# First weight pieces of the second pair issued on ScalarE's queue, layer 1's parameters loaded on the sync queue behind the lead

## The chip, the cores and the metric

The kernel runs on one core of one Trainium2 chip. The metric is the device time of one execution in microseconds (us). Before the change it was measured three times: 1794.83 us in the median, 1794.76 to 1796.19 us from end to end.

## What is computed

A trunk of two layers over 512 tokens of width 1024, all in float32. Each layer adds half of a SwiGLU feed-forward block, then a mixer (a convolution group beside differential attention, with one input and one output projection), then half of a second SwiGLU block:

```python
def rms_norm(x, g):
    xf = x.astype(jnp.float32)
    y = xf * lax.rsqrt(jnp.mean(xf * xf, axis=-1, keepdims=True) + EPS)
    return (y * g.astype(jnp.float32)).astype(x.dtype)

def swiglu(h, w_gate, w_up, w_down):
    return (jax.nn.silu(h @ w_gate) * (h @ w_up)) @ w_down

for l in range(DEPTH):
    x = x + 0.5 * swiglu(rms_norm(x, ffn1_norm[l]), ffn1_w_gate[l], ffn1_w_up[l], ffn1_w_down[l])
    h = rms_norm(x, mix_norm[l])
    ...
    x = x + jnp.concatenate([conv_out, diff_out], axis=-1) @ w_out[l]
    x = x + 0.5 * swiglu(rms_norm(x, ffn2_norm[l]), ffn2_w_gate[l], ffn2_w_up[l], ffn2_w_down[l])
```

D_FF is 2816, DEPTH is 2. The change lies in the first microseconds of layer 0's first `swiglu`.

## The kernel before

`x` is held transposed, as eight tiles of 128 features by 512 tokens (`x[:, k, :]`, k from 0 to 7). A product in float32 precision is made from three matmuls in the fp32r type: each operand is split into a high part and a rest, and `mm3` (L169 to L176) adds high by high (L172), rest of the activations by high weights (L175) and high activations by rest of the weights (L176). Weights come as raw float32 tiles `wraw`; `parts_of` (L96 to L101) makes their high part `whi` on ScalarE (L100; for the very first piece on VectorE, L98) and their rest `wlo` on VectorE (L101). `Prep.tile` (L258) does the same for the activations with the gain from the parameters: `acth` on ScalarE (L260), `actl` on VectorE (L261). The normalising factor is applied to the products afterwards, so the matmuls can start before it is known.

The first two of the 22 feed-forward blocks of 128 features are the lead. Each has a gate and an up weight tile, so there are four tiles of 128 by 1024 (512 KB), numbered n = 0 to 3 in the loop of L203; n = 0 and 1 are the first pair, n = 2 and 3 the second. The load loop of L200 brings them in three cuts: columns of k = 0 alone (64 KB for each tile), k = 1 to 3 (192 KB each), k = 4 to 7 (256 KB each), with the tiles of `x` between them. `lead_products` (L292) runs over k and, in each k, over the four tiles with three matmuls each: 12 matmuls for a k, 96 for the lead. Nine matmuls on ones (`ps_idle`, L196) run ahead of them, while the first data is on its way.

Plain loads are issued by SyncE (`nc.sync`) in program order, except the two parameter tables (`pars`, one for each layer, 128 by 159), which ScalarE issues first of all (L188). After them ScalarE loads its function table and runs one tiny activation on ones (L193). GpSimd issues the small loads of `make_scalars` and `make_bias` (L511, L491), which prepare scalars of both layers: they read `pars[0]` and `pars[1]` (L531, L535, L539, L542) and the table `lamv` (L517, multiplied on L519, reduced on VectorE, L521).

A scheduler places the instructions of each engine in an order that it computes from a model of their durations, so moving a load can reorder the instructions that use it. Each engine then works in its order, and an instruction that waits holds all behind it. Loads issued by SyncE and ScalarE share eight semaphores in turn, so a load's issue waits until the eighth load before it has landed.

Of the kernel before, what the change touches and what calls it, by code (L numbers as in the profile page):

```python
# [19 lines left out]
DEPTH = 2  # L20
# [47 lines left out]
def trunk(ctx: ExitStack, tc: tile.TileContext, xt, par, lamv, relb, onehot,  # L68
          gu1, dn1, wag, wqkv, wout, gu2, dn2, out):
    nc = tc.nc  # L70
# [25 lines left out]
    def parts_of(raw, hi, lo, eng=None, first=False):  # L96
        if first:
            V.tensor_scalar(hi, raw, 1.0, None, op0=ALU.mult)  # L98
        else:
            S.activation(hi, raw, AF.Copy)  # L100
        (eng or V).tensor_tensor(out=lo, in0=raw, in1=f32(hi), op=ALU.subtract)  # L101
# [81 lines left out]
    pars = []  # L183
    for l in range(DEPTH):
        pt = const.tile([P, NPAR], F32, tag=f"par{l}", name=f"par{l}")
        pars.append(pt)
    for l in range(DEPTH):
        nc.scalar.dma_start(pars[l], par[l])  # L188

    ones_r = const.tile([P, P + SPACE], F32R, tag="ones_r", name="ones_r")[:, :P]  # L190
    V.memset(f32(ones_r), 1.0)
# [8 lines left out]
    for k0, k1 in ((0, 1), (1, 4), (4, KT)):  # L200
        h = slice(k0 * P, k1 * P)
        nc.sync.dma_start(x[:, k0, :], xt[k0])
        for n, (raw, hi, lo) in enumerate(lead):  # L203
            nc.sync.dma_start(raw[:, h], gu1[0, n // 2, n % 2][:, h])
            parts_of(raw[:, h], hi[:, h], lo[:, h], first=k0 == n == 0)
        for k in range(k0 + 1, k1):
            nc.sync.dma_start(x[:, k, :], xt[k])
    lead = [[tuple(t[1:]) for t in lead[2 * m : 2 * m + 2]] for m in range(2)]
    ident = const.tile([P, P], F32, tag="ident", name="ident")
    make_identity(nc, ident)  # L210
# [725 lines left out]
```

## Time and profile before

| what | us |
|---|---|
| median of 3 runs | 1794.83 |
| lowest, highest | 1794.76, 1796.19 |
| profiled execution, its own time | 1795.22 |
| profiled execution, span from first to last instruction | 1793.4 |
| TensorE busy | 1783.9 |
| VectorE busy | 1199.0 |
| ScalarE busy | 896.4 |
| GpSimd busy | 646.6 |

The profiled execution is one run with the profiler; 1.8 us of its own time lie outside the span of its instructions, and its own time is 0.4 us above the median of the three. The granted TensorE clock was full throughout. In the rows below, PE is TensorE's matmuls, PEld its weight loads, DVE VectorE, ACT ScalarE, POOL GpSimd and SP SyncE; a "q" behind the engine marks what its sequencer issues. Rows of the timeline give the start, the duration from the first to the last of a merged group, the engine, the line, the operation with output and inputs, the count, and in brackets the idle time of the engine ahead of it with what ended it.

### The profile page before, as it was taken

What the parts mean: (1) busy time and instruction counts of PE and PEld (TensorE: products, weight loads), DVE (VectorE), ACT (ScalarE), POOL (GpSimd) and SP (SyncE); (2) the same over time, 40 slices, a digit from 0 to 9 for tenths busy, and PEclk for the clock granted to TensorE, in tenths of its full rate; (3) what the DMA queues carried; (4) which work ended last, traced back from release to release, by engine and by line L of the source; (5) the groups of instructions that cost most, each with busy time, mean ns of one, the idle gap of its engine ahead of it and who ended that gap; (6) DMA issues with size and microseconds to landing.
All of it is one profiled execution on the core that took longest, in us unless ns stands there. A gap on an engine that the chain in (4) does not pass through costs nothing.

```text
span 1793.4 us, 28370 instructions
## 1 busy us (share of the span) xinstructions
PE 1783.9 (99%) x10861; PEld 1590.7 (89%) x10861; DVE 1199.0 (67%) x1849; ACT 896.4 (50%) x1483; POOL 646.6 (36%) x453
## 2 busy tenths in 40 slices
PE   9999999999999999999999999999999999999999
PEld 7899899888788899899888998998887888998997
DVE  6966477568867867467566764765788587674762
ACT  6455265445744456256433543654558354552651
POOL 2243243269843133142102312412798331322420
PEclk9999999999999999999999999999999999999999
DMA  7376466323212366466334654663231133664751
GB/s 246 103 182 180 112 162 191 116 96 94 71 48 83 94 165 189 106 171 190 104 95 98 168 170 120 175 182 117 71 116 50 48 106 92 169 175 108 182 152 59
DMA packets 111721, 231.24 MB, mean 129 GB/s; under 512 B 12151, under 2 KB 33414, under 8 KB 111584
## 3 DMA queue, kind: packets, MB, share of 16 engines
q1 hardware_dynamic: 91488, 191.93, 33.2%
q0 software_dynamic: 19808, 37.33, 12.5%
q8 instruction: 85, 1.39, 0.3%
q14 instruction: 52, 0.43, 0.1%
q10 hardware_dynamic: 288, 0.16, 0.0%
HBM read 227.26 MB, written 3.42 MB: 129 GB/s over the span
## 4 chain that ended last, share of the span: by engine, by line
PE 95%; DVE 3%; issue 1%; DMA 0%; ACT 0%; SPq 0%; ACTq 0%; DVEq 0%
PE ps_pair L384 38%; PE ps_d L172 9%; PE ps_d L175 9%; PE ps_d L176 9%; PE ps_pair L176 5%; PE ps_pair L175 5%; PE ps_pair L172 5%; PE ps_pair L602 2%; PE ps_pair L601 2%; PE ps_pair L600 2%; PE ps_out L175 1%; PE ps_sc L718 1%; PE ps_out L176 1%; PE ps_out L172 1%; DVE actl L261 1%; PE ps_v L632 1%
## 5 line engine op out<-in xcount | busy, mean ns | idle before, releaser
L100 ACT ACTIVATE whi<-wraw 128x512 fp32r<-128x512 f32 (+2 forms) x600 | 466.4, 801 | 610.9 <-PE ps_pair L384 226.7
L101 DVE TENSOR_TENSOR wlo<-wraw,whi 128x512 fp32r<-128x512 f32 (+2 forms) x557 | 516.5, 950 | 225.3 <-ACT whi L100 220.6
L384 PE MATMUL ps_pair<-acth,wlo 128*128 128x256 f32 x1088 | 307.9, 283 | 0.0
L384 PE MATMUL ps_pair<-actl,whi 128*128 128x256 f32 x1088 | 307.9, 283 | 0.0
L384 PE MATMUL ps_pair<-acth,whi 128*128 128x256 f32 x1088 | 307.9, 283 | 0.0
L175 PE MATMUL ps_d<-hl,whi 128*128 128x512 f32 x704 | 274.0, 389 | 0.0
L176 PE MATMUL ps_d<-hh,wlo 128*128 128x512 f32 x704 | 272.9, 389 | 0.0
L172 PE MATMUL ps_d<-hh,whi 128*128 128x512 f32 x704 | 269.1, 389 | 0.0
L384 PE MATMUL ps_pair<-th,wlo 128*128 128x256 f32 x816 | 230.9, 283 | 0.0
L384 PE MATMUL ps_pair<-tl,whi 128*128 128x256 f32 x816 | 230.8, 283 | 0.0
L384 PE MATMUL ps_pair<-th,whi 128*128 128x256 f32 x816 | 230.8, 283 | 0.0
L150 POOL DMA_DIRECT2D wraw<-in_gu x68 | 81.9, 1204 | 408.3 <-DMA wraw<-in_gu 158.2
L155 POOL TENSOR_TENSOR wraw<-wraw 128x512 f32<-128x512 f32 x68 | 108.2, 1591 | 329.6 <-DMA wraw<-in_gu 242.8
L384 PEld LDWEIGHTS ps_pair<-acth,whi 128*128 128x128 f32 x1088 | 208.9, 192 | 0.3
L384 PEld LDWEIGHTS ps_pair<-actl,whi 128*128 128x128 f32 x1088 | 208.9, 192 | 0.3
L384 PEld LDWEIGHTS ps_pair<-acth,wlo 128*128 128x128 f32 x1088 | 208.9, 192 | 0.0
L484 DVE SCALAR_TENSOR_TENSOR x<-ps_d,x 128x512 f32<-128x512 f32 x96 | 64.8, 689 | 180.5 <-PE ps_d L176 180.1
L175 PE MATMUL ps_pair<-actl,whi 128*128 128x512 f32 x448 | 174.8, 391 | 0.3
L172 PE MATMUL ps_pair<-acth,whi 128*128 128x512 f32 x448 | 173.8, 392 | 1.3 <-ACT whi L100 1.3
L176 PE MATMUL ps_pair<-acth,wlo 128*128 128x512 f32 x448 | 174.3, 390 | 0.0
L384 PEld LDWEIGHTS ps_pair<-tl,whi 128*128 128x128 f32 x816 | 156.5, 192 | 0.7
L384 PEld LDWEIGHTS ps_pair<-th,whi 128*128 128x128 f32 x816 | 156.5, 192 | 0.6
(169 smaller groups left out, 3248.7 us busy)
## 6 DMA issues: line engine op xcount, KB each, us to landing
wraw<-in_gu SPq DMA_DIRECT2D x208, 256.0 KB, 4.0
wraw<-in_gu SPq DMA_DIRECT2D x104, 512.0 KB, 3.7
wraw<-in_gu POOLq DMA_DIRECT2D x68, 512.0 KB, 5.7
wraw<-in_wqkv SPq DMA_DIRECT2D x24, 512.0 KB, 3.7
wraw<-in_dn SPq DMA_DIRECT2D x84, 128.0 KB, 3.0
wraw<-in_dn SPq DMA_DIRECT2D x32, 256.0 KB, 3.2
wraw<-in_wag SPq DMA_DIRECT2D x16, 512.0 KB, 3.6
wraw<-in_wout SPq DMA_DIRECT2D x16, 512.0 KB, 3.6
```

The costliest lines, as they stand in the source:

```text
L100: S.activation(hi, raw, AF.Copy)
L101: (eng or V).tensor_tensor(out=lo, in0=raw, in1=f32(hi), op=ALU.subtract)
L150: nc.gpsimd.dma_start(two.rearrange("p (b c) -> p b c", b=2), u[:, h[0]].unsqueeze(1).broadcast_to([P, 2, 512]), accum_op=ALU.add)
L155: G.tensor_tensor(more[:, h[0]], two[:, h[1]], whole[:, h[0]], op=ALU.add)
L172: first = T.matmul(ps, wh, xh, start=start, stop=False)
L175: T.matmul(ps, wh, xl, start=False, stop=False)
L176: T.matmul(ps, wl, xh, start=False, stop=stop)
L384: mm = T.matmul(ps, l, r, start=first and i == j == 0, stop=False, skip_group_check=True)
L484: V.scalar_tensor_tensor(x[:, m, :], ps, 0.5, x[:, m, :], op0=ALU.mult, op1=ALU.add)
L600: T.matmul(ps[n], xh[:, t], wh, start=k == 0, stop=False)
L601: T.matmul(ps[n], xh[:, t], wl, start=False, stop=False)
L602: T.matmul(ps[n], xl[:, t], wh, start=False, stop=k == KT - 1)
```

## The change

Layer 0's parameters stay the first load on ScalarE's queue; layer 1's are issued by SyncE behind the last load of the lead. The first cuts (k = 0) of the two tiles of the second pair (n = 2 and 3) are issued on ScalarE's queue. In the program they come behind ScalarE's table load and its activation on ones.

```diff
-    for l in range(DEPTH):
-        nc.scalar.dma_start(pars[l], par[l])
+    nc.scalar.dma_start(pars[0], par[0])
...
     for k0, k1 in ((0, 1), (1, 4), (4, KT)):
         h = slice(k0 * P, k1 * P)
         nc.sync.dma_start(x[:, k0, :], xt[k0])
         for n, (raw, hi, lo) in enumerate(lead):
-            nc.sync.dma_start(raw[:, h], gu1[0, n // 2, n % 2][:, h])
+            (nc.scalar if k0 == 0 and n > 1 else nc.sync).dma_start(raw[:, h], gu1[0, n // 2, n % 2][:, h])
             parts_of(raw[:, h], hi[:, h], lo[:, h], first=k0 == n == 0)
         for k in range(k0 + 1, k1):
             nc.sync.dma_start(x[:, k, :], xt[k])
+    nc.sync.dma_start(pars[1], par[1])
```

No instruction of an engine is added or taken away; the number and the bytes of the loads stay the same.

## The prediction

> **What bounds the kernel now.** I read the page's first part, then TensorE's waits over the whole run, then the timeline of the first microseconds engine by engine.
>
> ```profile
> PE 1783.9 (99%) x10861; PEld 1590.7 (89%) x10861; DVE 1199.0 (67%) x1849; ACT 896.4 (50%) x1483; POOL 646.6 (36%) x453
> ```
>
> ```profile
> PE ps_at L739 <- ACT at L741: 1.3, 4, 0.4
> PE ps_pair L172 <- ACT whi L100: 1.3, 2, 0.9
> ```
>
> TensorE is busy for 99% of the span, and of its few waits only the second row lies in what the change touches: matmuls of the lead that wait for ScalarE to split a weight piece. TensorE's timeline shows where:
>
> ```profile
> 1.04 4.03 PE L196 MATMUL ps_idle<-ones_r 128*128 128x512 f32 x9 [1.04 <-DVE relb L493]
> 4.92 0.40 PE L172 MATMUL ps_pair<-acth,whi 128*128 128x512 f32 x1
> 5.70 0.50 PE L172 MATMUL ps_pair<-acth,whi 128*128 128x512 f32 x1 [0.38 <-ACT whi L100]
> ...
> 10.14 0.50 PE L172 MATMUL ps_pair<-acth,whi 128*128 128x512 f32 x1 [0.91 <-ACT whi L100]
> 10.48 0.39 PE L175 MATMUL ps_pair<-actl,whi 128*128 128x512 f32 x1
> 10.71 0.40 PE L176 MATMUL ps_pair<-acth,wlo 128*128 128x512 f32 x1
> 11.07 0.50 PE L172 MATMUL ps_pair<-acth,whi 128*128 128x512 f32 x1
> 11.42 0.40 PE L175 MATMUL ps_pair<-actl,whi 128*128 128x512 f32 x1
> ...
> 29.16 0.39 PE L172 MATMUL ps_pair<-acth,whi 128*128 128x512 f32 x1
> ```
>
> The matmul at 29.16 is the first after the lead's 96. Seventeen of the 96 ran before 11.07, so 79 ran from 11.07 on, and from 11.42 to 29.16 there are 78 steps in 17.74 us: 0.2274 us each, with no gap. The one at 11.07 took 0.35 to the next, 0.12 over a step, as does each that comes after a wait. From 4.92 to 29.16 are 24.24 us, and 96 steps are 21.83 us. **2.4 us is therefore all that the lead's waits cost**, 0.13% of the run. Everything behind 29.16 is TensorE's own queue and moves as a block.
>
> Now who is late. ScalarE's timeline:
>
> ```profile
> 0.72 0.89 ACTq L188 DMA_DIRECT2D par<-in_par  x2
> 1.65 1.28 ACT L193 ACT_TABLE_LOAD   x1 [1.65 <-PEq L925]
> 2.94 0.20 ACT L193 ACTIVATE warm<-ones_r 128x1 f32<-128x1 f32 x1
> 3.98 0.72 ACT L260 ACTIVATE acth<-x,par 128x512 fp32r<-128x512 f32 x1 [0.83 <-DMA par<-in_par]
> 5.33 0.88 ACT L100 ACTIVATE whi<-wraw 128x128 fp32r<-128x128 f32 x3 [0.64 <-DMA wraw<-in_gu]
> ...
> 7.79 0.51 ACT L100 ACTIVATE whi<-wraw 128x384 fp32r<-128x384 f32 x1
> 9.56 0.52 ACT L100 ACTIVATE whi<-wraw 128x384 fp32r<-128x384 f32 x1 [1.26 <-DMA wraw<-in_gu]
> 10.50 1.01 ACT L100 ACTIVATE whi<-wraw 128x384 fp32r<-128x384 f32 x2 [0.41 <-DMA wraw<-in_gu]
> ```
>
> Layer 0's parameters end the wait at 3.98; the k = 0 piece of n = 1 lands at 5.3; the 384-column pieces of n = 1 and n = 2 land at 9.55 and 10.5. These last two set the restart at 10.14 and the dense stretch from 11.07. SyncE's issues and the load on the DMA engines:
>
> ```profile
> 0.73 0.39 SPq L202 DMA_DIRECT2D x<-in_xt  x1
> 1.17 1.85 SPq L204 DMA_DIRECT2D wraw<-in_gu  x4
> 3.07 0.43 SPq L202 DMA_DIRECT2D x<-in_xt  x1
> 3.97 1.76 SPq L204 DMA_DIRECT2D wraw<-in_gu  x4
> ```
>
> ```profile
> SPq L204 <- DMA par<-in_par: 0.5, 1, 0.5
> ```
>
> ```profile
> 3.00:4.00 1.00, 1.00 (x4) 0.81 (x3) 0.00 (x0) 0.17 (x2) 0.08 (x1) 1.00 0.97 300
> 4.00:5.00 1.00, 1.00 (x4) 0.62 (x3) 0.79 (x3) 0.70 (x1) 0.67 (x4) 1.00 0.76 204
> 5.00:6.00 1.00, 0.62 (x3) 0.30 (x2) 0.78 (x2) 0.61 (x3) 1.00 (x2) 1.00 1.02 373
> 6.00:7.00 1.00, 1.00 (x6) 0.80 (x5) 0.95 (x3) 0.21 (x2) 0.93 (x5) 1.00 0.93 190
> 7.00:8.00 1.00, 1.00 (x6) 0.84 (x5) 0.28 (x3) 0.93 (x3) 0.79 (x4) 1.00 0.82 214
> ```
>
> The last two columns are the DMA engines' busy share and GB/s. From 3 us on they are nearly full; the issuing is not what holds the bytes back. From 6 to 8 they are as busy but move only about 200 GB/s: the 384-column pieces go slowly there, for a reason that the trace does not give.
>
> **The change part by part.** Landings come from these rows:
>
> ```profile
> x<-in_xt SPq DMA_DIRECT2D x2, 256.0 KB, 3.2
> wraw<-in_gu SPq DMA_DIRECT2D x4, 64.0 KB, 3.4
> par<-in_par ACTq DMA_DIRECT2D x2, 79.5 KB, 3.2
> ```
>
> *ScalarE's front.* One issue of 0.45 (half of 0.89) goes, so the table load starts at 1.2 and the activation on ones ends at 2.7; then come two weight issues, at 2.7 and 3.15, where SyncE issued them at 2.1 and 2.55 (third and fourth of four in 1.85). ScalarE is free at 3.6 instead of 3.14, which costs nothing: it waits anyway, until 3.98 before and longer now. With 3.4 to landing, n = 2 and 3 arrive at 6.1 and 6.55; by the median of before they arrived near 5.5 and 5.95. So these two pieces come later, not earlier.
>
> *SyncE's front.* Two issues less put x tile 1 at 2.1 (before 3.07) and the first 384-column piece at 2.55 (before 3.97). That piece waited for the parameters' landing, being the eighth load after it; now the second 384-column piece does, at 3.97 instead of about 4.4. The pieces of n = 1, 2 and 3 are thus issued some 0.45 earlier.
>
> *What that is worth at landing.* With the engines full, an earlier issue brings only their slack: 0.24 us in the stretch from 4 to 5. Layer 1's parameters no longer stand in front: 79.5 KB at 300 GB/s, 0.27 us. Together 0.5 us: the 384-column pieces of n = 1 and 2 land at 9.05 and 10.0, the k = 0 piece of n = 1 at about 4.95 (of the 0.5, the 0.27 and half of the slack). Bounds: nothing at all (9.55), since full engines may give the time back elsewhere; or, if the slow stretch from 6 to 8 is the pieces' meeting with other traffic and goes, a landing of 384-column n = 1 by 7.5, its issue plus 3.4. I take 9.05, near the first, because nothing in the change makes fewer bytes than one small table.
>
> The Trainium skill speaks against the first half of this: "DMA: Bandwidth & Descriptors", section "Issuing engines are not separate DMA queues", says that issuing from several engines saves no more than the issuing engine's own time, since all loads run on the same 16 DMA engines. The full rows above agree with it as far as they go. By it alone the 0.24 falls away and the sum below would end at about -0.1.
>
> *The order on the engines*, as the changed kernel is built, is the part against. ScalarE now splits n = 1's first piece **before** it makes `acth` of x tile 0. Before, `acth` ran at 3.98, as soon as the parameters were there; now it waits behind a piece that lands at 4.95. Then: split 0.29 (0.88 by three), `acth` 0.72, end 5.96, first lead matmul at 6.05 instead of 4.92. From there TensorE has work: the next two matmuls need splits of n = 1 (made) and n = 2 (landed 6.1, made by 6.4, matmul at 6.5); `actl`, 0.75, is ready at 6.75. ScalarE goes on with `acth` of x tile 1 (landed near 5.5; to 7.1), n = 3 (to 7.4) and the first 384 columns (to 7.9, needed at 6.05 + 11 x 0.2274 = 8.55). The twelfth matmul is that one; the thirteenth needs n = 1's 384 columns: 9.05 + 0.52 + 0.05 = 9.62, a wait of 0.8. The following pieces (10.0 + 0.52 = 10.5) arrive inside the five steps after that. Dense from 9.62, 84 matmuls: 0.35 + 83 x 0.2274 = 19.22, so the lead ends at 28.84 instead of 29.16. **Sum: -0.3 us.**
>
> *Layer 1's parameters.* They arrive behind the lead, near 18. Their readers on GpSimd are off the path by this row:
>
> ```profile
> POOL oneh L498 <- DVE ssum L273: 11.1, 1, 11.1
> ...
> POOL lamv L519 <- DMA lamv<-in_lamv: 5.9, 1, 5.9
> ```
>
> GpSimd idles 11.1 us until 27.6 ahead of the next thing it has to wait for, and the moved work there is some 2 us. Without that cover a late table would hold `make_bias`. SyncE's extra issue, 0.45 at about 13, delays loads that are first needed at 29.16; no cost. But GpSimd's order changes: the second `lamv` load, 128 KB, no longer stands behind layer 1's scalars.
>
> ```profile
> 9.38 0.62 POOL L517 DMA_DIRECT2D lamv<-in_lamv  x1
> ```
>
> It is issued about 2 us sooner, near 7.4, and its bytes meet the 384-column pieces and x tiles 2 to 4. Cost: 128 KB at 204 to 373 GB/s is 0.35 to 0.65 us on pieces that TensorE waits for, if they queue behind it; nothing if they are through by then. I take nothing for the sum, as the pieces of n = 1 and 2 are queued earlier, and keep 0.65 for the range.
>
> Against the profiled execution the sum is 1795.22 - 0.3 = 1794.9; that execution stands 0.4 above the median, so the forecast is 1794.5.
>
> **Rivals.** *A: the slow stretch goes.* Pieces land by 7.5 to 8.5, TensorE runs dense from the first lead matmul at 5.95: 5.95 + 0.12 + 96 x 0.2274 = 27.9, -1.3, or 1793.5. For it: the wait of 0.91 and most of the 2.4 come from that stretch, and its traffic is rearranged. Against: the bytes in front of it are nearly the same, and the first matmul's later start caps the gain.
>
> *B: ScalarE's new order decides, slower.* If the 384-column pieces land no sooner than before, TensorE restarts at 10.14 as before, but with 12 matmuls done instead of 14: 10.14 + 0.35 + 83 x 0.2274 = 29.36, +0.2. From there every microsecond of later landing adds one: with the `lamv` load ahead of them, +0.65, it is +0.85, or 1795.7; with the slow stretch as long as 9.55 - 7.5 = 2.05 moved on by half, +1.2 to +1.7. For it: full DMA engines and a first matmul 1.1 us later. Against: 80 KB less in front. It decides as soon as n = 1's 384 columns land after 9.4.
>
> *C: TensorE falls to the rate of the idle matmuls.* Nine took 4.03, 0.448 each, about twice a lead step. The lead now leaves TensorE idle for some 1.0 us behind them. If that brought the slow rate back for the twelve matmuls up to the next wait, it would cost 12 x 0.22 = 2.6, of which the wait of 0.8 absorbs its part: +1.5 in all, 1796.3. Against: after the 0.91 idle before 10.14 the matmuls kept full pace. The Trainium skill, "TensorE: Matmul & The Clock Gate", Part 1, has the slow rate return only after an idle window of about 3.4 us, which the gap here does not fill; by that too it stays away.
>
> **How the numbers follow.** Forecast (-0.9 to 0): 0.50. A: 0.15. B: 0.28. C: 0.04. Something not seen here: 0.03. What a measurement of this kernel can tell from no change is 0.2%, 3.6 us, more than the whole purse of 2.4, so A, B and C by themselves all fall within it; only B with C together or the unseen reach beyond: slower 0.04, faster 0.03, same 0.93. The range: A's 1793.5 less 0.5 for its landings, 1793.0, up to B's +1.7 with 0.5 of the 1.4 us between the runs of before, 1797.0.
>
> **What would show it.** Right: the first lead matmul near 6.0, one long wait for n = 1's 384 columns ending near 9.6, the matmul that is at 29.16 near 28.85, and the rest of the run unchanged in length. Wrong: that piece landing before 8 (A) or after 9.4 (B), lead matmuls above 0.23 apart (C), a first matmul near 4.9 (the order does not matter), or a difference that first appears behind 30 us.

## The result, and the profile after

The changed kernel takes 1797.14 us in the median of 22 runs (1795.03 to 1798.95); the kernel before takes 1794.51 us in 22 runs (1793.89 to 1796.19) beside them. The ratio is 1.0015, with a 95% interval from 1.0009 to 1.0021: slower by 2.6 us, clear of noise, within the 0.2% that the prediction called no change, and 0.1 us above the top of its range. The sign was forecast the other way. The runs of after also scatter by 3.9 us, those of before by 2.3. In the text, "before" and "after" are the two kernels, and "the ones" are the matmuls on ones ahead of the lead.

The profiled execution of after is its slowest, 1798.95 us with a span of 1797.2, so its rows show more than the median loss. All of the 3.73 us between the two spans (1797.18 and 1793.45 before rounding) is there by the end of the lead. The four small matmuls on L230, inside the third block's gate product, make a landmark. TensorE's timeline before and after has them here:

```profile
31.88 0.60 PE L230 MATMUL ps_rows<-ident,ssum 128*128 128x128 f32 x4
```

```profile
35.58 0.60 PE L230 MATMUL ps_rows<-ident,ssum 128*128 128x128 f32 x4
```

That is 3.70 later; from there to the end both need 1761.6 us. So only the start has to be explained. ScalarE's timeline after:

```profile
0.72 0.41 ACTq L187 DMA_DIRECT2D par<-in_par  x1
1.16 1.28 ACT L192 ACT_TABLE_LOAD   x1 [1.16 <-PEq L925]
1.23 0.88 ACTq L203 DMA_DIRECT2D wraw<-in_gu  x2
2.46 0.20 ACT L192 ACTIVATE warm<-ones_r 128x1 f32<-128x1 f32 x1
7.25 0.31 ACT L100 ACTIVATE whi<-wraw 128x128 fp32r<-128x128 f32 x1 [4.59 <-DMA wraw<-in_gu]
7.46 0.70 ACT L260 ACTIVATE acth<-x,par 128x512 fp32r<-128x512 f32 x1
```

ScalarE waits 4.59 us for n = 1's first piece, and `acth` of x tile 0, whose inputs had landed by 4.05, stands behind it. The two weight pieces on ScalarE's queue are issued from 1.23 on, beside the table load. TensorE's timeline:

```profile
1.04 3.66 PE L195 MATMUL ps_idle<-ones_r 128*128 128x512 f32 x9 [1.04 <-DVE relb L493]
8.22 1.65 PE L172 MATMUL ps_pair<-acth,whi 128*128 128x512 f32 x3 [3.52 <-ACT acth L260]
9.67 0.63 PE L175 MATMUL ps_pair<-actl,whi 128*128 128x512 f32 x1
10.09 0.63 PE L176 MATMUL ps_pair<-acth,wlo 128*128 128x512 f32 x1
...
32.86 0.39 PE L172 MATMUL ps_pair<-acth,whi 128*128 128x512 f32 x1
```

The first lead matmul is at 8.22 (4.92 before), and the following ones are 0.43 apart instead of 0.227. The row at 32.86 is the one that stood at 29.16. In stretches of 5 us, the column ahead of the last two is the granted clock:

```profile
5.00:10.00 5.00, 1.78 (x4) 1.49 (x5) 2.09 (x6) 2.75 (x8) 1.89 (x7) 0.73 0.93 274
10.00:15.00 5.00, 5.00 (x15) 3.88 (x14) 4.23 (x10) 3.48 (x8) 0.28 (x1) 0.58 0.95 263
15.00:20.00 5.00, 5.00 (x24) 4.14 (x23) 2.23 (x6) 2.03 (x5) 0.60 (x2) 1.00 1.00 363
```

At half rate, 0.73 and 0.58 stand for 2.7 and 4.2 us of half clock, 6.9 us in all; it ends near 14.2, where the steps fall from 0.43 to 0.23. The lead took 24.64 us from its first matmul (32.86 - 8.22), 2.8 more than 96 steps of 0.2274. Before it took 24.24. So the half clock took the place of the waits for data, 2.8 against 2.4, and the late start of 3.30 (8.22 - 4.92) came on top: 3.30 + 0.4 = 3.7.

### The profile page after: what moved, and what is told of

The parts are those of the page before. It is cut to its first block, busy times and chain, and to the rows that moved or that the text cites. A ratio compares the mean times of both kernels' runs of the same rounds, so it can differ in the third digit from the quotient of the medians.

```text
span 1797.2 us, 28370 instructions
## 1 busy us (share of the span) xinstructions
PE 1785.5 (99%) x10861; PEld 1593.1 (89%) x10861; DVE 1196.0 (67%) x1849; ACT 895.4 (50%) x1483; POOL 640.2 (36%) x453
## 4 chain that ended last, share of the span: by engine, by line
PE 95%; DVE 3%; issue 1%; ACT 0%; DMA 0%; SPq 0%; ACTq 0%; DVEq 0%
PE ps_pair L384 38%; PE ps_d L175 9%; PE ps_d L176 9%; PE ps_d L172 9%; PE ps_pair L175 5%; PE ps_pair L172 5%; PE ps_pair L176 5%; PE ps_pair L601 2%; PE ps_pair L602 2%; PE ps_pair L600 2%; PE ps_out L175 1%; PE ps_sc L718 1%; PE ps_out L176 1%; PE ps_out L172 1%; DVE actl L261 1%; PE ps_v L630 1%
## 5 line engine op out<-in xcount | busy, mean ns | idle before, releaser
L155 POOL TENSOR_TENSOR wraw<-wraw 128x512 f32<-128x512 f32 x68 | 102.7, 1510 | 322.7 <-DMA wraw<-in_gu 271.1
```

What stands on the lines that cost most here:

```text
L155: G.tensor_tensor(more[:, h[0]], two[:, h[1]], whole[:, h[0]], op=ALU.add)
```

## The experiments

Each run is timed in five rounds beside the kernel before on its chip. The median of the latter was 1794.29 us for the first four runs of the table, 1794.38 for the next four and 1794.34 for the last four. The expectations speak of theory O (ScalarE's order decides) and its rival T (the loads issued sooner make pieces late in whatever order), and of theory L (GpSimd's lambda load holds the piece) and its rival X (x tile 1 and the 384-column pieces do). Profiles are of single executions; "piece n = 1" is the second tile's 64 KB piece. The landings are those of its last part: a load lands in 16 parts, whose times the trace has.

| kernel | median us (11 runs) | lowest to highest | piece n = 1 landed (profile) | first lead matmul |
|---|---|---|---|---|
| after_again | 1796.82 | 1794.18 to 1797.80 | 6.27 | 7.27 |
| only_params | 1795.17 | 1794.74 to 1796.03 | 4.74 | 4.97 |
| only_queue | 1795.01 | 1794.54 to 1797.82 | 5.79 | 6.79 |
| order_fix | 1794.96 | 1793.89 to 1798.60 | 5.79 | 5.05 |
| more_idle | 1796.67 | 1796.20 to 1797.52 | 5.81 | 9.22 |
| lamv_sync | 1794.93 | 1794.19 to 1796.27 | 4.58 | 5.57 |
| order_lamv | 1794.48 | 1794.28 to 1798.92 | 5.54 | 4.96 |
| before_lamv | 1794.55 | 1794.02 to 1795.24 | 4.43 | 5.05 |
| idle14 | 1796.19 | 1794.85 to 1798.20 | 5.76 | 6.76 |
| order_idle14 | 1794.94 | 1794.13 to 1796.29 | 5.85 | 6.26 |
| params_lamv | 1794.34 | 1793.85 to 1794.95 | 4.33 | 5.05 |
| swap_only | 1795.10 | 1794.46 to 1796.26 | 5.35 | 6.35 |

**after_again**: the changed kernel unaltered.

> The changed kernel, unaltered, looked at once more. In its first profile the first lead matmul came at 8.22 us, behind ScalarE's split of the second tile's first piece (which landed at 7.2), and TensorE ran at half its clock from 7.3 to 14.2. If the lateness of that piece is fixed by the traffic, first lead matmul again near 8.2 and the time near 1798.9. If it varies from run to run, the first lead matmul lies anywhere between 6 and 8.5, the half clock comes only where it lies beyond some 8, and the times spread over 1795 to 1799 with a median near 1797.

Its profile is milder, 1795.0 us of span:

```profile
7.27 1.35 PE L172 MATMUL ps_pair<-acth,whi 128*128 128x512 f32 x3 [2.43 <-ACT acth L260]
```

```profile
5.00:10.00 5.00, 2.73 (x7) 2.17 (x8) 3.05 (x8) 3.68 (x10) 2.17 (x6) 0.77 0.95 327
10.00:15.00 5.00, 5.00 (x21) 4.03 (x21) 3.37 (x7) 2.74 (x4) 0.00 (x0) 0.89 0.90 286
```

The first lead matmul is at 7.27 and the half clock lasts 3.4 us (2.3 + 1.1) instead of 6.9. The piece's lateness thus varies from execution to execution. The half clock came already with an idle stretch of 2.4, sooner than expected (only beyond a first lead matmul at some 8). Of the 33 runs of the changed kernel in both sets, 22 have a mean granted clock of 0.999 or 0.998. Seven more are below 1796.7 at 1.000, and four lie at 1798.1 to 1798.8 at 1.000. What these four may be, the next run suggests; none of them was profiled.

**swap_only**: all loads as before; ScalarE held to the order of after. The edit is against the kernel before.

```diff
+            parts_of(raw[:, h], hi[:, h], lo[:, h], first=k0 == n == 0, pin=k0 == 0 and n == 1)
+            if k0 == 0 and n == 1:
...
+                tc.keep_in_program_order(S.activation(acth[:, 0, :], x[:, 0, :], AF.Copy, scale=g0))
...
```

> The kernel before the change, all loads as they were, but ScalarE held to the second tile's split ahead of acth of x tile 0, as in the changed kernel. The order by itself: first lead matmul at 6.1 to 6.4 instead of 4.9, no half clock since TensorE idles only some 1.3 us, 1794.5 to 1795.2, so at most 0.9 of the loss. If the order alone makes the whole loss: 1796.5 or more.

Measured 1795.10, 0.8 above before (ratio 1.0005, 0.9996 to 1.0014: inside the noise by its interval), as expected of an order that is at most 0.9 of the loss. So the order alone is not the whole loss. The first lead matmul, at 6.35, is as expected too. Its profile holds a surprise:

```profile
1.04 4.21 PE L198 MATMUL ps_idle<-ones_r 128*128 128x512 f32 x9 [1.04 <-DVE relb L502]
6.35 2.08 PE L174 MATMUL ps_pair<-acth,whi 128*128 128x512 f32 x4 [1.10 <-ACT acth L211]
8.22 0.63 PE L177 MATMUL ps_pair<-actl,whi 128*128 128x512 f32 x1
```

```profile
5.00:10.00 5.00, 3.90 (x10) 2.88 (x10) 3.59 (x9) 3.71 (x9) 4.59 (x11) 1.00 0.95 299
```

The matmuls run at 0.43 a step until 10.4, though the granted clock reads 1.00: in this execution the ones did not bring the full clock up, and the record of the clock, on which the column rests, begins only when it does. A clock of 1.00 in that column therefore does not exclude half-rate matmuls at the start; the steps have to be read.

**order_fix**: both edits, with `acth` of x tile 0 held ahead of the split of piece n = 1. The edit is against the changed kernel.

```diff
+        if k0 == 0:
+            g0 = pars[0][:, _AT["ffn1_norm"] : _AT["ffn1_norm"] + 1]
+            tc.keep_in_program_order(S.activation(acth[:, 0, :], x[:, 0, :], AF.Copy, scale=g0))
...
-    for k in range(KT):
+    for k in range(1, KT):
         pr.tile(k, squares=False)
```

> Both edits of the change, but ScalarE is held to acth of x tile 0 ahead of the second tile's split; loads and queues as in the changed kernel. Theory O: first lead matmul near 4.9, three matmuls done before the second tile is needed, full clock, and the loss of 2.6 us gone: 1793.5 to 1795. Rival T: the pieces land as late as in the changed kernel and TensorE waits for them instead, some 2 to 3 us behind the first three matmuls, 1796 to 1798.

The median falls by 1.9 against after_again, to 1794.96, and the profile (1793.97) is one of the fastest of the study:

```profile
5.05 0.44 PE L174 MATMUL ps_pair<-acth,whi 128*128 128x512 f32 x1
6.17 0.74 PE L174 MATMUL ps_pair<-acth,whi 128*128 128x512 f32 x2 [0.68 <-ACT whi L100]
```

The first matmul comes at 5.05, the second waits for piece n = 1 until 6.17, and from there TensorE is dense: the 384-column pieces keep ahead of it, as the prediction's early issue had it. But four of the eleven runs lie at 1797.4 to 1798.6, so the order is not the whole of it either: the ratio to before is 1.0009 (1.0000 to 1.0018), that of after_again 1.0013 (1.0004 to 1.0022). The gain of the order by itself is therefore in the median and in the profile, but not shown clear of the noise.

**idle14** and **order_idle14**: `IDLE = 14` instead of 9, in the changed kernel and in order_fix. **more_idle**: `IDLE = 25` in the changed kernel.

> The changed kernel with 25 matmuls on ones ahead of the lead instead of 9, so that TensorE stays at work until about 8 us. If the half clock is a part of the loss of its own (in the first profile of the changed kernel it took 13 steps at 0.427 us instead of 0.227, 2.6 us): no half clock after the start, lead steps of 0.227 from the first on, the first lead matmul where it was (7 to 8.2, or when the ones end), 1795.0 to 1796.0 and a spread of about 1. Rival (the late pieces alone cost it, the half clock only fills waits that would come anyway): waits of 2 us appear behind the first lead matmul and the time stays near 1797.

> The changed kernel with 14 matmuls on ones instead of 9. They end near 6.1 to 6.5 us, before ScalarE's split and acth allow the first lead matmul in most executions (6.8 to 8.2 in the profiles so far), so unlike the 25 they hold back nothing. If the half clock is a loss of its own: lead steps of 0.227 behind the first lead matmul, no execution with a mean granted clock of 0.999 or less, median 1795.0 to 1795.8 instead of 1796.8 to 1797.1. If the late piece alone costs the time: median 1796.5 or more.

> As the last, with acth of x tile 0 ahead of the second tile's split. The order alone gave 1793.9 to 1795.6 in seven executions and 1797.4 to 1798.6 in four. If these four are executions in which TensorE's clock came up late (the first matmuls ran at half rate), they vanish with more matmuls on ones: 1793.9 to 1795.6, median near 1794.6. If they come from a piece that lands several us late, they stay, some four of eleven above 1797.

With 25 the time missed the expected 1795.0 to 1796.0, and the ones themselves held the lead:

```profile
1.04 8.34 PE L195 MATMUL ps_idle<-ones_r 128*128 128x512 f32 x25 [1.04 <-DVE relb L493]
9.22 0.85 PE L172 MATMUL ps_pair<-acth,whi 128*128 128x512 f32 x3
```

The lead starts at 9.22, where `acth` of x tile 0 (6.05 to 6.76) had been ready since about 6.8, and then runs without one gap at 0.227 to the landmark at 33.74. Its 24.5 us from the first matmul to the landmark compare with 27.4 in the profile of after: the half clock's 2.8, once it is gone. The time stayed at 1796.67 because the 25 ones gave that back: in the profile of after_again the lead begins at 7.27.

With 14 the median is 1796.19, 0.6 and 1.0 below the two medians of the changed kernel; one run of eleven has a clock of 0.999, where most had. The expectation of 1795.0 to 1795.8 was missed. The late piece may cost more than I gave it, but the profiled execution is the fastest of the eleven (1794.85) and does not show what held the others. So the half clock's 2.8 us is read from profiles; no median shows it, and the 0.6 to 1.0 here is not clear of the noise (ratio to before 1.0010, 1.0000 to 1.0019). In order_idle14 the four runs above 1797 are gone (highest 1796.29), as expected of executions in which the clock comes up late; the median, 1794.94, is no lower than with the order alone, as the ones run until the first lead matmul at 6.26, which had come at 5.05. That the four runs of order_fix were such executions is an inference from this and from swap_only's profile; none of the four was profiled. It does not fit all of them: one, 1797.37, has a mean granted clock of 0.999, so its clock had come up and fallen again.

**lamv_sync**: the changed kernel with the lambda loads, 128 KB each, moved from GpSimd's queue to the sync queue, where they come behind the lead.

```diff
-            nc.gpsimd.dma_start(lv, lamv[l].partition_broadcast(P))
+            nc.sync.dma_start(lv, lamv[l].partition_broadcast(P))
```

> The changed kernel with both loads of the lambda vectors taken from GpSimd's queue to the sync queue behind the lead. In four profiles the last parts of the second tile's first piece landed together with the last parts of the first lambda load (7.05 and 7.23; 6.12 and 6.27; 5.23 and 4.74; 5.67 and 5.79). Theory L (the lambda load's slow packets hold the DMA engines that carry the piece): the piece lands by 5.0 with all its 16 parts within 0.6, first lead matmul near 6, no half clock, 1793.0 to 1794.5 with a spread below 1.5. Rival X (x tile 1 and the 384-column pieces, issued 1 us sooner, hold it): it still lands at 5.8 to 7.3, first lead matmul at 6.8 to 8.3, median 1796 or more.

```profile
4.60 0.31 ACT L100 ACTIVATE whi<-wraw 128x128 fp32r<-128x128 f32 x1 [1.94 <-DMA wraw<-in_gu]
4.81 0.71 ACT L260 ACTIVATE acth<-x,par 128x512 fp32r<-128x512 f32 x1
```

```profile
5.57 0.98 PE L172 MATMUL ps_pair<-acth,whi 128*128 128x512 f32 x3 [0.46 <-ACT acth L260]
```

Piece n = 1 lands at 4.58, all of its 16 parts between 4.31 and 4.58, as theory L had it. In the profile of after, thirteen parts landed by 4.75 and three at 6.96 to 7.23; the last three parts of the lambda load landed at 6.79 to 7.05. With the load out of the way the first lead matmul comes at 5.57 in spite of the order, no run has a mean granted clock below 1.00, and the median is 1794.93, 1.9 below after_again and still above the 1793.0 to 1794.5 expected. Behind the landmark this build needs 1762.1 instead of 1761.6, which is 0.5 of what is left against before. Of this, 0.37 lies behind the last matmul, and the four builds with the lambda loads moved all have it: SyncE closes the kernel with nine waits for semaphores, 0.06 us each, and with two more loads in the turn of eight the last store's comes third and not last, so that six waits follow its landing. This part says nothing about the start.

**order_lamv**, **before_lamv**, **params_lamv**: the same edit on order_fix, on the kernel before and on only_params.

> As the last, and ScalarE held to acth of x tile 0 ahead of the second tile's split. Theories O and L together: first lead matmul near 5.0, second tile ready by 5.3, waits of less than 1 us in the lead, no half clock: 1792.0 to 1793.5, about 1 to 2 us faster than before the change, without the upper cluster of 1797 to 1798.6 that the order alone left. Rival X: the upper cluster stays.

> The kernel before the change with the lambda loads on the sync queue behind the lead. Theory L: its 384-column piece of the second tile, which landed at 9.5, is not behind the lambda load (that had landed at 5.1), so little changes there; the first pieces come up to 0.4 sooner: 1793.0 to 1794.2. Rival X: no change, 1794.3.

> Only layer 1's parameters moved, and the lambda loads on the sync queue behind the lead. The parameters alone gave 1795.17, 0.9 above before, and their profile had a wait of 1.7 us at 16.5 behind VectorE's reduction of the second lambda load, which stands ahead of actl in VectorE's order there. If that wait is the 0.9: the reduction is out of the lead and the median is 1794.2 to 1794.7. If not: 1795 again.

The first missed its 1792.0 to 1793.5: 1794.48, equal to before (ratio 1.0003, 0.9994 to 1.0012). Its 0.5 behind the landmark takes a part; in its profile piece n = 1 came at 5.54, its 384-column piece only at 9.47, and TensorE waited 0.45 at 10.07. So pieces can be late without the lambda load, too. One run of eleven, 1798.92, stayed up, and its cause is open. The second came out at 1794.55, as said for theory X, no change. The third is at 1794.34, 0.8 below only_params.

**only_params** and **only_queue**: one edit of the two. Both are shown, in this order, against the changed kernel.

```diff
-            (nc.scalar if k0 == 0 and n > 1 else nc.sync).dma_start(raw[:, h], gu1[0, n // 2, n % 2][:, h])
+            nc.sync.dma_start(raw[:, h], gu1[0, n // 2, n % 2][:, h])
```

```diff
-    nc.scalar.dma_start(pars[0], par[0])
+    for l in range(DEPTH):
+        nc.scalar.dma_start(pars[l], par[l])
...
-    nc.sync.dma_start(pars[1], par[1])
```

> Only layer 1's parameters move; all four first pieces stay on the sync queue. ScalarE then makes acth of x tile 0 ahead of the second tile's split, as before the change. Theory O (ScalarE's order decides): first lead matmul near 4.9 as before, full clock, 1794.2 to 1795.0, same as before within 0.5 us. Rival T (earlier traffic makes pieces late in whatever order): the 384-column pieces are issued about 0.5 earlier here too, so some of the loss shows, 1795.5 or more.

> Only the second pair's first pieces go to ScalarE's queue; both parameter tables stay ahead of them. ScalarE's order is that of the changed kernel: split of the second tile's piece ahead of acth of x tile 0. Both theories: slower than before, 1796 to 1798, first lead matmul after 6. Theory O has that wait, and the half clock where it grows beyond 3 us, make all of the loss; if instead the time is that of before within 0.5, neither the order nor the queue but the two edits together are at fault.

The parameters alone cost 0.9 (1795.17), the queue alone 0.7 (1795.01, with four of eleven runs at 1796.2 to 1797.8); both intervals reach below no change. Both together cost 2.5. The queue alone was expected at 1796 to 1798 and is mostly below. Its profile, of one of its longer runs (1796.65), has the late piece and the half clock as well, after an idle stretch of only 1.9:

```profile
6.79 0.96 PE L172 MATMUL ps_pair<-acth,whi 128*128 128x512 f32 x3 [1.90 <-ACT acth L260]
```

The parameters alone fall between theory O (up to 1795.0) and rival T (from 1795.5). In the profile of only_params the lead starts in time and a wait stands further back:

```profile
15.54 0.29 DVE L521 TENSOR_REDUCE lamd<-lamv 128x2 f32<-128x128 f32 x1 [4.25 <-POOL lamv L519]
15.75 0.74 DVE L261 SCALAR_TENSOR_TENSOR actl<-x,par,acth 128x512 fp32r<-128x512 f32 x1
```

```profile
16.54 0.50 PE L175 MATMUL ps_pair<-actl,whi 128*128 128x512 f32 x1 [1.31 <-DVE actl L261]
```

VectorE stands 4.25 us at the reduction of the second lambda load, `actl` of an x tile waits behind it, and TensorE for that. With the lambda loads behind the lead's (params_lamv) VectorE stands only 0.78 us at the first reduction, at 20.52, TensorE has no such wait, and the 0.8 is gone. The edit also clears the lambda load from the first microseconds, so this run does not part the two.

## Why the prediction was wrong

**What bounded the kernel, and where the change can act: right.** Everything behind the landmark took within 0.1 of 1761.6 us before, after, and in each variant that left the lambda loads alone. The 2.4 us of waits bounded what could be won; the loss had no such bound, and the prediction used it for both sides. Its 3.6 us that could be told from no change was too coarse as well: 22 runs each told 2.6 us with an interval of 0.06% to either side. Against the forecast of 28.84 for the first matmul behind the lead, the profile of after has 32.86: 2.2 of the 4.0 are the start (8.22 instead of 6.05), 1.8 the lead's length (24.64 instead of 22.79).

**The landing of piece n = 1: wrong, and the main step that failed.** The prediction put it at "about 4.95", and worked out first lead matmul and order from there. In the seven profiles with the early issues and the lambda load in place it landed between 5.76 and 7.23. Landings in the profiles, by what is issued around it:

| | lambda load at 1.34 | lambda load behind the lead |
|---|---|---|
| x tile 1 issued near 3.05 | 4.74, 5.31, 5.35 | 4.33, 4.43 |
| x tile 1 issued near 2.1, two pieces on ScalarE's queue | 5.76 to 7.23 (seven) | 4.58, 5.54 |

The gain that the prediction gave the 80 KB less in front may be real (4.74 in only_params against 5.31 and 5.35 in before and swap_only), but something larger goes the other way. By the table this is the earlier issue of the other loads together with GpSimd's lambda load, which hold the last parts of the piece. That most of the loss goes when the lambda loads go is shown by the eleven runs of lamv_sync. That it is by the piece's landing, and how the two hold it, rests on single profiles, and 5.54 without the lambda load says that the early issue can do a part of it alone. I had looked for GpSimd's traffic only in its second lambda load, and bounded the 384-column pieces, not this one. The Trainium skill, "DMA: Bandwidth & Descriptors", section "Queues, rings and completion order", says that an engine's completion mark lands only after all its earlier writes, those of other queues included. That fits parts of the piece landing just behind parts of the lambda load (7.05 and 7.23; 6.12 and 6.27), though no run here shows the ordering itself; in others the piece came first (6.56 and 5.81).

**ScalarE's order: right in kind.** That `acth` would wait behind the split, and the first lead matmul come late by it, was in the working and in rival B. Measured alone (swap_only) it costs 0.8 by the medians, inside the noise; with the late piece it makes the start 3.3 later in the profile of after.

**The half clock: rival C, dismissed at 0.04.** Its condition was read from the forecast's own gap, "some 1.0 us", instead of from the gap that a late piece would give. The two are not independent: the later the piece, the longer the idle stretch. The gap was 3.52 and 2.43 us in the two profiles of after and 1.90 in that of only_queue, and all three have the half clock; a gap of 1.31 (only_params, at 16.54) brought none. In each of the three, the trace's record of the clock has it come up and fall 3.41 us later (3.91 and 7.33, 4.24 and 7.65, 4.31 and 7.72), and the half clock last 3.41 us or twice that. TensorE was idle for 2.6, 2.4 and 1.9 us of the 3.41 between. So in these profiles no gap of 3.4 us was needed: it was enough that TensorE idled for more than half of one such stretch. Its price was nearly right: 2.8 against 2.6. The window of about 3.4 us that the prediction takes from the Trainium skill ("TensorE: Matmul & The Clock Gate", Part 1) agrees in size with the 3.41 of the record. It was used wrongly as a safe limit on the gap, and here the measurement decides: a gap of 1.90 was enough in one execution, and in swap_only nine matmuls on ones had not brought the clock up at all.

**ScalarE's front: wrong, without effect on the sign.** The two issues were put at 2.7 and 3.15, behind the table load. They came at 1.23 and 1.65, beside it; n = 2 landed earlier than before (4.48 against 5.68), n = 3 later (7.54 against 5.87). The forecast of 6.1 and 6.55 missed both.

**The 384-column pieces: right.** Forecast at 9.05 and 10.0 for n = 1 and 2, landed at 8.94 and 9.44. But TensorE, late and at half rate, no longer waited for them, so nothing was won by it.

**Layer 1's parameters: right for GpSimd, incomplete.** GpSimd was through with them at 24.2 and then idled another 4.41 us. The second lambda load went out at 7.44 in only_params, as forecast (7.4), but at 9.65 in after. That the reordering can put VectorE's reduction of this load ahead of `actl` was missed; by its profile and by params_lamv it is most of the 0.9 of only_params, though neither the 0.9 nor the 0.8 that params_lamv takes away is clear of the noise by the intervals against before.

**The range** ended at B's +1.7 with some scatter. B and C together were named and left outside, and what happened is near to them, but not by B's condition: n = 1's 384 columns landed at 8.94, ahead of the 9.4 from which B should decide, and it was the 64 KB piece that came late. B's own terms add up to more than the +1.7: 0.2 for the restart, 0.65 for the lambda load and 1.03 for half of the 2.05 are 1.88. With that the range would have reached 1797.2 and held the median, but by luck.

## What to carry to other kernels

Where a load moves forward, look at what lands last among everything issued around it, on all queues, and at what the engine's order puts behind that landing: here one 64 KB piece, late beside a 128 KB load of another queue, stopped a ready activation and with it TensorE. Treat a delay of TensorE and its fall to half clock as one mechanism. Matmuls on ones can cover the wait, but they do not shorten it: here 14 and 25 of them left the changed kernel at 1796.19 and 1796.67. No version here beats the kernel before beyond the noise; the fastest medians, 1794.34 and 1794.48, equal it.

## What was not expected of the hardware

The same kernel's piece landed at 7.23 in one execution and 6.27 in another, from the same issue at 1.64. Loads on ScalarE's queue are issued while its table load of 1.28 us still runs (1.23 in 1.16 to 2.44). Nine matmuls on ones from 1.04 on usually end with the full clock up (between 3.9 and 5.3 us in nine profiles), but in two of the eleven profiles with nine ones it came at 7.1 (before_lamv) and 10.4 (swap_only), and the mean granted clock did not show it. In the profile of before, too, the record of the clock begins only at 4.74, so the full clock that it reports holds from there on.
